# Neighbourhood attention: how q, k and v are laid out in scratch memory and loaded

## The chip, the cores and the metric

The kernel runs on one core of one Trainium2 chip. The metric is the device time of one execution in microseconds. The kernel before was run three times: 3532.39, 3535.32 and 3536.39 us, median 3535.32 us.

## What is computed

An encoder layer over two sequences, one of 512 tokens (prompt, s = 0) and one of 2048 (sample, s = 1), width 1024, all in float32. After a layer norm the input is projected by w_in into the operands of four mixers of width 256; their outputs are joined, projected by w_out, and followed by a layer norm, a feed-forward block with a convolution of width 3, and a last layer norm. The change touches the first mixer, neighbourhood attention: tokens stand on a grid with rows of 64, and each query attends to a window of 8 rows by 16 columns, with a bias by relative place.

```python
def _mixer(h, ...):
    z = h @ w_in
    ...
    o_a = _natten(qa.reshape(hs), ka.reshape(hs), va.reshape(hs), na_rpb)
    o_b = _fourier_mix(fb)
    o_c = _mla(cq, ckv, kr, mla_q_g, w_uq, mla_kv_g, w_ukv, cos, sin)
    o_d = _spatial_gating(sg, sgu_ln_g, sgu_ln_b, sgu_w, sgu_b)
    mix = jnp.concatenate([o_a, o_b, o_c, o_d], axis=-1)
    return mix @ w_out
```

## The kernel before, in words

The program runs in stages, and intermediate results pass between them through scratch tensors in HBM. To keep float32 precision, an operand x is split into a high part (rounded to fp32r) and a low part, x minus the high part; a product is then the sum of three matmuls, or of two in which both parts stand on 128 partitions, 64 for each. hi() at L126 and L130 and split() at L136 make the parts: L126 is ScalarE (ACT), L130 GpSimd (POOL), L136 VectorE (DVE) or POOL.

**First phase (phase1, 0 to about 500 us).** Five blocks of 512 tokens. feat() (L386) computes 128 features for a block: f 0 and 1 are q (two pairs of heads j), 2 and 3 are k, 6 and 7 feed the Fourier mixer. It empties PSUM into two tiles of the tag zs (four buffers), hi and lo, and stores them: q goes to zq[s][j] as three planes, hi, lo, hi; k to zk[s][j] as two planes. keyed() (L417) computes the values, tokens on the partitions, 128 tokens at a time, and stores one tile zs of 128 rows by 2 KB (both pairs, both heads, hi and lo) to zv[s].

**Attention stage.** From about 680 us natten() (L655) and mla() (L844, the third mixer) run woven together: the loop in build() takes three steps of natten for every four of mla. natten works in bands of eight grid rows of queries, two for the prompt and eight for the sample (s, j, i), and each band in eight units: four ranges of columns c (starting at CW = 0, 8, 24, 32, each 32 wide) by two heads hh. For a unit, scores() multiplies q by k (L708), adds the bias table and takes the maximum on DVE (L711), does the exponential on ACT and scales on POOL (L717); flip() transposes on TensorE (L726); values() multiplies by the values (L738, L739). The loads:

- band(): for each head hh, q is a tile of 128 partitions: partitions 0 to 63 hold one part, 64 to 127 the other. Two loads fill it (x = 0 straight, x = 1 with the parts exchanged, by taking planes x and x + 1 of the three); one load fills k (kt in the code, a tile of the arena, so a<-zk in the trace). The source pattern of each is 2 planes by 64 rows by columns. It is called six units ahead.
- window(): the values of one range of columns, in loads of 128 rows by 1 KB; the source pattern is 4 grid rows by 32 columns by 256 values. It is called two units ahead.
- table(): the bias table of a unit (L692 on), a load of 8 by 16 by n values from the scratch tensor R into one of six tiles tbl, then an addition of the mask on POOL at L697. It is called three units ahead; the ranges c = 1 and 2 share a table. The mask has one buffer and is loaded once a band.

In mla(), softmax() scales a row block of scores on POOL at L924, and turn() transposes it on TensorE at L936 afterwards. Its own loads go into a ring of three tiles raw.

**What sets the order.** Each engine works through its own instructions in order, in the order in which the program emits them and a scheduler places them. All loads and stores are issued by the SyncE queue (SP), through load() at L118 and store() at L121, so one that waits for a buffer, or whose issue takes long, holds all behind it.

Of the kernel before, what the change touches and what calls it, by code (L numbers as in the profile page):

```python
# [9 lines left out]
F32 = mybir.dt.float32  # L10
# [5 lines left out]
P = 128  # L16
D = 1024
KD = D // P
SEQS = ((0, 512), (1, 2048))
# [3 lines left out]
GRID_W = 64  # L23
# [8 lines left out]
CW = (0, 8, 24, 32)  # L32
# [74 lines left out]
class Builder:  # L107
# [65 lines left out]
    def build(self):  # L173
        tc, nc, I = self.tc, self.nc, self.I
        with tc.tile_pool(name="cst", bufs=1, reuse_waits="tile") as cst, tc.tile_pool(name="scr", bufs=1, space=bass.MemoryType.DRAM) as scr:
# [20 lines left out]

            d = lambda shape, tag: self.t(scr, shape, tag)
            self.y1 = [d([T, D], f"y1_{s}") for s, T in SEQS]
            self.zq = [[d([3, P, T], f"zq{s}_{j}") for j in range(2)] for s, T in SEQS]
            self.zk = [[d([2, P, T], f"zk{s}_{j}") for j in range(2)] for s, T in SEQS]  # L200
            self.zv = [d([T, 2, 2, 2, 64], f"zv{s}") for s, T in SEQS]
            self.zf = [[d([2, P, T], f"zf{s}_{j}") for j in range(2)] for s, T in SEQS]
            self.c = [d([3, P, T], f"c{s}") for s, T in SEQS]
            self.kr = [d([T, 32], f"kr_{s}") for s, T in SEQS]
# [64 lines left out]
    def phase1(self):  # L269
        tc, nc, I = self.tc, self.nc, self.I  # L270
        w_in = I["w_in"][0].rearrange("(k p) n -> p k n", p=P)
        with tc.tile_pool(name="p1w", bufs=1, reuse_waits="tile") as wp, tc.tile_pool(name="p1x", bufs=1, reuse_waits="tile") as xp, \
# [113 lines left out]
            def feat(b, f, uT):  # L386
                s, t0 = blocks[b]
                xh, xl = xT[b]
                ps = self.t(pp, [P, 512], "mm", bufs=4)
                for k in range(KD):  # L390
                    self.mm3(ps, wh[f][:, k], wl[f][:, k], xh[k], xl[k], k == 0, k == KD - 1)
                if f < 8:
                    hi = self.t(sp, [P, 512], "zs", F32R, bufs=ZS)
                    lo = self.t(sp, [P, 512], "zs", F32R, bufs=ZS)
                    j = f % 2
                    if f < 2:
                        src = ps.rearrange("p (r c q) -> p c r q", r=8, c=4, q=16)
                        dh, dl = [a.rearrange("p (c r q) -> p c r q", c=4, q=16)[:, :, ::-1, ::-1] for a in (hi, lo)]
                        self.split(src, dh, dl, "act", "dve")
                        dst = self.zq[s][j]  # L400
                    elif f < 4:
                        nc.scalar.activation(hi, ps, AF.Copy, scale=-0.125)
                        nc.vector.scalar_tensor_tensor(lo, ps, -0.125, hi.bitcast(F32), op0=ALU.mult, op1=ALU.subtract)
                        dst = self.zk[s][j]
                    else:
                        self.evac(ps, hi, lo)
                        dst = self.zf[s][j]
                    for i, a in enumerate((hi, lo, hi) if f < 2 else (hi, lo)):
                        self.store(dst[i, :, t0:t0 + 512], a.bitcast(F32))
                elif f < 11:  # L410
                    zs = self.t(sp, [P, 512], "zs", bufs=ZS)
                    nc.scalar.copy(zs, ps)
                    self.store(self.c[s][f - 8][:, t0:t0 + 512], zs)
                else:
                    nc.scalar.activation(uT[:, f - 11], ps, AF.Gelu_apprx_tanh)

            def keyed(b):  # L417
                s, t0 = blocks[b]
                xh, xl = xT[b]
                for t2 in range(2):  # L420
                    ps = self.t(pp, [P, 2, 2 * P], "mm", bufs=4)
                    for t in range(2):
                        tl = slice((2 * t2 + t) * P, (2 * t2 + t + 1) * P)
                        for k in range(KD):
                            self.mm3(ps[:, t], xh[k][:, tl], xl[k][:, tl], vh[:, k], vl[:, k], k == 0, k == KD - 1)
                    for t in range(2):
                        z = self.t(sp, [P, 2, 2, 2, 64], "zs", F32R, bufs=ZS)
                        src = ps[:, t].rearrange("p (j h d) -> p j h d", j=2, h=2)
                        self.split(src, z[:, :, :, 0], z[:, :, :, 1], "act", "dve")
                        r0 = t0 + (2 * t2 + t) * P  # L430
                        self.store(self.zv[s][r0:r0 + P].rearrange("p j h a d -> p (j h a d)"),
                                   z.bitcast(F32).rearrange("p j h a d -> p (j h a d)"))

            def keep_wout(k):
                wo = I["w_out"][0].rearrange("(k p) (a n) -> p k a n", p=P, a=2)
# [7 lines left out]
            def token(b):  # L443
                s, t0 = blocks[b]
                xh, xl = xT[b]
                v = self.t(xp, [P, 4, 4, 64], "uv", bufs=2)
                krs = self.t(sp, [P, 4, 32], "krs", bufs=1)
                vps = [self.t(pp, [P, 288], "mm", bufs=4) for _ in range(4)]
                for k in range(KD):
                    wk, wlk = wh[13][:, k], wl[13][:, k]  # L450
                    for t in range(4):
                        tl = slice(t * P, (t + 1) * P)
                        nc.tensor.matmul(vps[t], xh[k][:, tl], wk, start=k == 0, stop=False)
                        nc.tensor.matmul(vps[t], xh[k][:, tl], wlk, start=False, stop=False)
                        nc.tensor.matmul(vps[t], xl[k][:, tl], wk, start=False, stop=k == KD - 1)
                for t in range(4):
                    nc.scalar.activation(v[:, t].rearrange("p h d -> p (h d)"), vps[t][:, :256], AF.Gelu_apprx_tanh)
                    nc.scalar.copy(krs[:, t], vps[t][:, 256:288])
                self.store(self.kr[s][t0:t0 + 512].rearrange("(t p) e -> p t e", p=P), krs)
                return v  # L460
# [37 lines left out]
            for b in range(nb):  # L498
                uv = lambda: self.t(xp, [P, 2, 512], "uv", bufs=2)
                if b < nb - 1:  # L500
                    for f in range(3):
                        feat(b, f, None)
                    norm(b + 1)
                    feat(b, 3, None)
                    keyed(b)
                    for f in range(6, 11):
                        feat(b, f, None)
                        if b and wo:
                            keep_wout(wo.pop(0))
                    uT = uv()  # L510
                    for f in range(11, 13):
                        feat(b, f, uT)
                    v = token(b)
                    turn(b + 1)
                    gating(b, v, uT)
                else:
                    v = token(b)
                    uT = uv()
                    for f in range(11, 13):
                        feat(b, f, uT)  # L520
                    for f in range(2):
                        feat(b, f, None)
                    gating(b, v, uT)
                    for f in (2, 3):
                        feat(b, f, None)
                    keyed(b)
                    for f in range(6, 11):
                        feat(b, f, None)
# [126 lines left out]
    def natten(self, wp):  # L655
# [6 lines left out]
        half = (slice(0, 64), slice(64, P))  # L662

        def band(s, j, i):
            _, r0, nr = BANDS[s][i]
            n = nr * GRID_W
            kt = self.a((10, 12)[jobs.index((s, j, i)) % 2], [P, 2, 1024], F32R)
            for hh in range(2):
                q = self.t(wp, [P, 2, 4, P], "q", F32R, bufs=4)
                for x in range(2):  # L670
                    self.load(q[:, x].bitcast(F32).rearrange("p c q -> p (c q)"),
                              self.zq[s][j][x:x + 2, half[hh], i * 512:(i + 1) * 512])
                self.load(kt[:, hh, :n].bitcast(F32), self.zk[s][j][:, half[hh], r0 * GRID_W:r0 * GRID_W + n])
                qk[s, j, i, hh] = q, kt[:, hh]

        def window(s, j, i, c):
            _, r0, nr = BANDS[s][i]
            v = self.t(wp, [P, 4, 2, P], "vt", F32R, bufs=3)
            z = self.zv[s]
            for k in range(nr // 4):  # L680
                self.load(v[:, k].bitcast(F32).rearrange("p h d -> p (h d)"),
                          bass.AP(z.tensor, z.offset + ((r0 + 4 * k) * GRID_W + CW[c]) * 512 + j * 256,
                                  [[GRID_W * 512, 4], [512, 32], [1, 256]]))
            V[s, j, i, c] = v

        def table(s, j, i, c, hh):
# [65 lines left out]
        N, LAG = len(units), 2  # L752
        at = lambda f, x: f(units[x]) if 0 <= x < N else None
        band(*jobs[0])
        window(*units[0][:4])
        for x in range(3):
            table(*units[x])
# [833 lines left out]
```

## Time and profile before

| | |
|---|---|
| median of three runs | 3535.32 us |
| profiled execution, its own time | 3535.3 us |
| its span | 3533.5 us |
| busy: PE, DVE, ACT, POOL | 3141.0, 2119.8, 1375.6, 1620.1 us |
| mean granted clock of TensorE | 0.94 |
| moved by DMA | 653.42 MB, mean 185 GB/s |

The span is the time between the first and the last instruction recorded; the profiled execution's own time is 1.8 us longer. PE is TensorE's matmul, PEld its weight load. SPq is the SyncE queue: the time of one of its rows is that of issuing a DMA, not of moving the data. A matmul's recorded duration overlaps its neighbours' (they are pipelined), so counts of matmuls in a stretch say more of the pace than their durations. The granted clock is 1.00 at full speed (2.4 GHz) and 0.50 at the lower level (1.2 GHz); a value between is a mean over the stretch. The DMA share is the mean over the core's 16 DMA engines.

### The profile page before, as it was taken

To read this page: it belongs to the slowest core of one execution; us is meant where nothing else is said; L and a number is where in the kernel's file an instruction comes from. 1 tells how busy PE (TensorE), PEld (TensorE's weight loads), DVE (VectorE), ACT (ScalarE), POOL (GpSimd) and SP (SyncE) were. 2 spreads that over 40 slices of the span, in tenths; PEclk is the share of its full clock that TensorE was granted. 3 is DMA by queue.
4 is the path that set the end of the run, shared out by engine and by line. 5 is a ranking of instruction groups with operands and counts; after the bars stand their busy time and mean duration, and the time that the engine had idled before them with its cause. 6 is when DMAs were issued, how large, how long until landed. Compare 5 with 4: busy or idle time off the path is not lost. (4 is left out here: it accounts for less than half of the span.)

```text
span 3533.5 us, 46949 instructions
## 1 busy us (share of the span) xinstructions
PE 3141.0 (89%) x16375; PEld 2752.1 (78%) x16375; DVE 2119.8 (60%) x3802; ACT 1375.6 (39%) x2497; POOL 1620.1 (46%) x1360
## 2 busy tenths in 40 slices
PE   7999999555567666999999999999989999999997
PEld 6788888445566556888878998898979997787785
DVE  6333235444455455765478787666556556769678
ACT  3222234433344444652244444443344332225324
POOL 6322114423444333643378875655244213456546
PEclk9999999677788788999999999999999999999999
DMA  7354263222222222245466666999769867667653
GB/s 240 139 184 162 65 216 123 83 77 72 96 90 81 87 84 88 68 139 170 150 221 238 241 238 235 325 330 327 250 220 355 270 232 263 226 214 269 216 189 125
DMA packets 410432, 653.42 MB, mean 185 GB/s; under 512 B 50512, under 2 KB 266928, under 8 KB 409428
## 3 DMA queue, kind: packets, MB, share of 16 engines
q1 hardware_dynamic: 410196, 650.43, 53.5%
q8 instruction: 130, 2.13, 0.2%
q14 instruction: 106, 0.87, 0.1%
HBM read 437.31 MB, written 213.00 MB: 184 GB/s over the span
## 5 line engine op out<-in xcount | busy, mean ns | idle before, releaser
L136 POOL TENSOR_TENSOR w<-wraw,w 128x512 fp32r<-128x512 f32 x150 | 225.6, 1507 | 325.1 <-ACT w L126 281.1
L936 PE MATMUL t<-ident,a 128*128 128x128 f32 x1088 | 174.6, 292 | 138.1 <-POOL a L924 135.2
L908 DVE TENSOR_SCALAR_CACHE_REDUCE a<-s,low 128x512 f32<-128x512 f32 x272 | 195.3, 744 | 155.8 <-PE s L145 148.9
L1247 PE MATMUL s<-B,w 128*128 128x450 f32 (+1 forms) x792 | 284.7, 362 | 2.9 <-DVE h L1117 2.1
L1248 PE MATMUL s<-B,w 128*128 128x450 f32 (+1 forms) x792 | 286.1, 361 | 0.5 <-DVE B L136 0.5
L1248 PE MATMUL t<-T,w 128*128 128x450 f32 (+1 forms) x792 | 285.2, 360 | 0.0
L1247 PE MATMUL t<-T,w 128*128 128x450 f32 (+1 forms) x792 | 281.0, 360 | 3.9 <-DVE u L1117 3.5
L1249 PE MATMUL s<-B,w 128*128 128x450 f32 (+1 forms) x792 | 284.5, 359 | 0.0
L1249 PE MATMUL t<-T,w 128*128 128x450 f32 (+1 forms) x792 | 283.3, 358 | 0.0
L936 PEld LDWEIGHTS t<-ident,a 128*128 128x128 f32 x1088 | 138.9, 151 | 161.6 <-POOL a L924 138.8
L697 POOL TENSOR_TENSOR tbl<-tbl,mask 128x384 f32<-128x384 f32 (+2 forms) x60 | 63.2, 1056 | 393.9 <-DMA tbl<-R 355.8
L136 DVE TENSOR_TENSOR a<-t,a 128x512 fp32r<-128x512 f32 x240 | 160.1, 684 | 120.0 <-ACT a L126 118.4
L126 ACT CAST a<-t 128x512 fp32r<-128x512 f32 x240 | 136.1, 587 | 228.9 <-PE t L936 224.9
L1255 DVE SCALAR_TENSOR_TENSOR h<-h,convc,h 128x896 f32<-128x896 f32 (+1 forms) x132 | 221.5, 1708 | 0.0
L952 PE MATMUL o<-a,a 128*128 128x256 f32 x544 | 149.9, 301 | 56.7 <-ACT a L126 52.2
L1254 DVE SCALAR_TENSOR_TENSOR h<-h,convc,h 128x896 f32<-128x896 f32 (+1 forms) x132 | 166.5, 1292 | 54.0 <-ACT h L1253 54.0
L1453 PE MATMUL t<-w,go 128*128 128x512 f32 x696 | 194.8, 399 | 4.2 <-ACT go L126 1.8
L1253 ACT ACTIVATE h<-h,convc 128x896 f32<-128x896 f32 (+1 forms) x132 | 138.3, 1095 | 129.7 <-DVE h L1117 128.7
L144 PE MATMUL mm<-xTl,a 128*128 128x512 f32 x440 | 174.6, 397 | 1.5 <-DVE xTl L136 1.5
L953 PE MATMUL o<-a,a 128*128 128x256 f32 x544 | 155.2, 315 | 20.9 <-POOL a L136 20.5
L126 ACT CAST w<-wraw 128x512 fp32r<-128x512 f32 x154 | 94.9, 618 | 198.3 <-PE t L1249 135.7
L145 PE MATMUL mm<-xTh,a 128*128 128x512 f32 x440 | 171.2, 393 | 0.0
(366 smaller groups left out, 9363.4 us busy)
## 6 DMA issues: line engine op xcount, KB each, us to landing
w<-wuops SPq DMA_DIRECT2D x220, 512.0 KB
wuops<-w SPq DMA_DIRECT2D x110, 512.0 KB
w<-wdops SPq DMA_DIRECT2D x104, 512.0 KB
wraw<-in_w_up_dram SPq DMA_DIRECT2D x88, 512.0 KB
wdops<-xs SPq DMA_DIRECT2D x74, 512.0 KB
graw<-g SPq DMA_DIRECT2D x100, 256.0 KB
wd<-wdops SPq DMA_DIRECT2D x48, 512.0 KB
g<-h SPq DMA_DIRECT2D x44, 448.0 KB
```

Source lines behind the costliest of these rows:

```text
L126: nc.scalar.copy(out, src)
L136: e.tensor_tensor(lo, src, hi.bitcast(F32), op=ALU.subtract)
L144: mm(ps, wh, xl, start=False, stop=False)
L145: mm(ps, wl, xh, start=False, stop=last)
L908: nc.vector.tensor_scalar(e[:, c * 512:c * 512 + 512], ps, 1.0, self.low, op0=ALU.mult, op1=ALU.max, accum_out=m4[:, c:c + 1])
L936: nc.tensor.transpose(pt[:, k], e[:, kk * P:(kk + 1) * P], self.ident)
L1247: mm(ps[:, :hw], a, xh, start=first and k == 0, stop=False, skip_group_check=True)
L1248: mm(ps[:, :hw], a, xl, start=False, stop=False, skip_group_check=True)
L1249: mm(ps[:, :hw], b, xh, start=False, stop=last and k == KH - 1, skip_group_check=True)
L1254: nc.vector.scalar_tensor_tensor(c[:, :n], hb[:, 1:n + 1], cw[:, 1, ft:ft + 1], c[:, :n], op0=ALU.mult, op1=ALU.add)
L1255: nc.vector.scalar_tensor_tensor(c[:, :n], hb[:, 2:n + 2], cw[:, 2, ft:ft + 1], c[:, :n], op0=ALU.mult, op1=ALU.add)
L1453: mm = lambda a, b, st, sp_: nc.tensor.matmul(ps, a, b, start=st, stop=sp_, skip_group_check=True)
```

## The change

zq keeps two planes (hi, lo) in place of three. band() loads each half of 64 partitions by itself: four loads for a head's q, two for its k. zv is replaced by one scratch tensor for each range of columns c, whose rows stand in the order in which window() reads them: two grid rows (128 tokens) give 64 rows. keyed() stores each tile of values in eight pieces of 32 rows, one for each range and grid row; the ranges overlap. window() then loads 128 rows that lie one after the other.

```diff
--- before.py
+++ after.py
@@ -196,9 +196,9 @@
 
             d = lambda shape, tag: self.t(scr, shape, tag)
             self.y1 = [d([T, D], f"y1_{s}") for s, T in SEQS]
-            self.zq = [[d([3, P, T], f"zq{s}_{j}") for j in range(2)] for s, T in SEQS]
+            self.zq = [[d([2, P, T], f"zq{s}_{j}") for j in range(2)] for s, T in SEQS]
             self.zk = [[d([2, P, T], f"zk{s}_{j}") for j in range(2)] for s, T in SEQS]
-            self.zv = [d([T, 2, 2, 2, 64], f"zv{s}") for s, T in SEQS]
+            self.zv = [[d([T // 2, 2, 2, 2, 64], f"zv{s}_{c}") for c in range(4)] for s, T in SEQS]
             self.zf = [[d([2, P, T], f"zf{s}_{j}") for j in range(2)] for s, T in SEQS]
             self.c = [d([3, P, T], f"c{s}") for s, T in SEQS]
             self.kr = [d([T, 32], f"kr_{s}") for s, T in SEQS]
@@ -405,7 +405,7 @@
                     else:
                         self.evac(ps, hi, lo)
                         dst = self.zf[s][j]
-                    for i, a in enumerate((hi, lo, hi) if f < 2 else (hi, lo)):
+                    for i, a in enumerate((hi, lo)):
                         self.store(dst[i, :, t0:t0 + 512], a.bitcast(F32))
                 elif f < 11:
                     zs = self.t(sp, [P, 512], "zs", bufs=ZS)
@@ -427,9 +427,12 @@
                         z = self.t(sp, [P, 2, 2, 2, 64], "zs", F32R, bufs=ZS)
                         src = ps[:, t].rearrange("p (j h d) -> p j h d", j=2, h=2)
                         self.split(src, z[:, :, :, 0], z[:, :, :, 1], "act", "dve")
-                        r0 = t0 + (2 * t2 + t) * P
-                        self.store(self.zv[s][r0:r0 + P].rearrange("p j h a d -> p (j h a d)"),
-                                   z.bitcast(F32).rearrange("p j h a d -> p (j h a d)"))
+                        r0 = (t0 + (2 * t2 + t) * P) // 2
+                        zz = z.bitcast(F32).rearrange("p j h a d -> p (j h a d)")
+                        for c in range(4):
+                            for r in range(2):
+                                self.store(self.zv[s][c][r0 + 32 * r:r0 + 32 * r + 32].rearrange("p j h a d -> p (j h a d)"),
+                                           zz[64 * r + CW[c]:64 * r + CW[c] + 32])
 
             def keep_wout(k):
                 wo = I["w_out"][0].rearrange("(k p) (a n) -> p k a n", p=P, a=2)
@@ -667,20 +670,18 @@
             kt = self.a((10, 12)[jobs.index((s, j, i)) % 2], [P, 2, 1024], F32R)
             for hh in range(2):
                 q = self.t(wp, [P, 2, 4, P], "q", F32R, bufs=4)
-                for x in range(2):
-                    self.load(q[:, x].bitcast(F32).rearrange("p c q -> p (c q)"),
-                              self.zq[s][j][x:x + 2, half[hh], i * 512:(i + 1) * 512])
-                self.load(kt[:, hh, :n].bitcast(F32), self.zk[s][j][:, half[hh], r0 * GRID_W:r0 * GRID_W + n])
+                for a in range(2):
+                    for x in range(2):
+                        self.load(q[half[a], x].bitcast(F32).rearrange("p c q -> p (c q)"),
+                                  self.zq[s][j][a ^ x, half[hh], i * 512:(i + 1) * 512])
+                    self.load(kt[half[a], hh, :n].bitcast(F32), self.zk[s][j][a, half[hh], r0 * GRID_W:r0 * GRID_W + n])
                 qk[s, j, i, hh] = q, kt[:, hh]
 
         def window(s, j, i, c):
             _, r0, nr = BANDS[s][i]
             v = self.t(wp, [P, 4, 2, P], "vt", F32R, bufs=3)
-            z = self.zv[s]
             for k in range(nr // 4):
-                self.load(v[:, k].bitcast(F32).rearrange("p h d -> p (h d)"),
-                          bass.AP(z.tensor, z.offset + ((r0 + 4 * k) * GRID_W + CW[c]) * 512 + j * 256,
-                                  [[GRID_W * 512, 4], [512, 32], [1, 256]]))
+                self.load(v[:, k].bitcast(F32).rearrange("p h (a d) -> p h a d", a=2), self.zv[s][c][(r0 + 4 * k) * 32:(r0 + 4 * k + 4) * 32, j])
             V[s, j, i, c] = v
 
         def table(s, j, i, c, hh):
```

## Rows read from the trace of the kernel before

**Rows 1.** The page, the span in 40 slices of 88 us: busy tenths, granted clock.

```profile
PE   7999999555567666999999999999989999999997
...
PEclk9999999677788788999999999999999999999999
DMA  7354263222222222245466666999769867667653
```

**Rows 2.** Waits, 690 to 1470 us: who waited for whom; total us, times, longest.

```profile
POOL tbl L697 <- DMA tbl<-R: 355.8, 32, 37.6
...
PE t L936 <- POOL a L924: 135.2, 10, 31.2
```

**Rows 3.** Timeline of POOL: start, duration, instruction; in brackets idle time before, releaser.

```profile
710.47 2.90 POOL L697 TENSOR_TENSOR tbl<-tbl,mask 128x256 f32<-128x256 f32 x4 [25.85 <-DMA tbl<-R]
...
882.55 0.99 POOL L697 TENSOR_TENSOR tbl<-tbl,mask 128x384 f32<-128x384 f32 x1 [32.03 <-DMA tbl<-R]
...
1016.85 1.27 POOL L697 TENSOR_TENSOR tbl<-tbl,mask 128x512 f32<-128x512 f32 x1 [10.67 <-DMA tbl<-R]
...
1348.73 1.26 POOL L697 TENSOR_TENSOR tbl<-tbl,mask 128x512 f32<-128x512 f32 x1 [7.90 <-DMA tbl<-R]
...
1381.85 1.26 POOL L697 TENSOR_TENSOR tbl<-tbl,mask 128x512 f32<-128x512 f32 x1 [28.07 <-DMA tbl<-R]
```

**Rows 4.** Timeline of the SyncE queue, 840 to 866 us.

```profile
842.76 1.82 SPq L118 DMA_DIRECT2D a<-zk  x1
844.62 12.30 SPq L118 DMA_DIRECT2D q<-zq  x2
856.97 5.32 SPq L118 DMA_DIRECT2D a<-zk  x1
862.39 3.56 SPq L118 DMA_DIRECT2D tbl<-R  x1
```

**Rows 5.** Short windows: length, busy us and count by engine, granted clock, DMA share, GB/s.

```profile
850.00:856.00 6.00, 6.00 (x35) 5.42 (x34) 3.10 (x10) 1.82 (x6) 0.52 (x2) 0.72 0.13 52
...
868.00:874.00 6.00, 0.00 (x0) 0.00 (x0) 0.00 (x0) 0.00 (x0) 0.00 (x0) 0.50 0.26 90
...
1505.00:1520.00 15.00, 14.80 (x106) 13.40 (x105) 12.48 (x37) 10.37 (x15) 6.95 (x6) 1.00 1.00 385
```

**Rows 6.** Eight windows without band loads in the way: two of them, and the sum.

```profile
980.00:1020.00 40.00, 38.78 (x264) 34.97 (x263) 33.12 (x94) 27.53 (x52) 18.11 (x20) 0.96 0.27 90
1060.00:1082.00 22.00, 21.79 (x154) 19.57 (x153) 17.97 (x50) 16.60 (x30) 12.86 (x13) 1.00 0.29 84
...
sum 175.00, PE 171.54 PEld 154.22 DVE 147.26 ACT 127.43 POOL 91.41; mean PE 21.44 PEld 19.28 DVE 18.41 ACT 15.93 POOL 11.43
```

**Rows 7.** Timeline of PE near 1350 us.

```profile
1351.99 1.11 PE L936 MATMUL t<-ident,a 128*128 128x128 f32 x4 [7.58 <-POOL a L924]
```

**Rows 8.** Windows of the stage: its start, the whole of it, its tail.

```profile
690.00:745.00 55.00, 21.16 (x78) 15.32 (x78) 12.56 (x43) 10.04 (x20) 8.70 (x12) 0.59 0.27 84
690.00:1423.00 733.00, 461.56 (x2839) 404.98 (x2839) 361.15 (x1059) 312.47 (x602) 278.60 (x286) 0.79 0.26 85
...
1423.00:1500.00 77.00, 72.85 (x474) 64.91 (x472) 57.21 (x167) 51.69 (x98) 44.17 (x44) 0.93 0.20 59
```

**Rows 9.** By tile, issues on SP: ns min/median/max, first and last start.

```profile
L118 SPq DMA_DIRECT2D q<-zq x40: 500/2643/11733, 681.1 to 1351.7; - x40
...
L118 SPq DMA_DIRECT2D a<-zk x20: 495/1724/9567, 602.4 to 1358.2; - x20
...
L118 SPq DMA_DIRECT2D vt<-zv x128: 514/544/5074, 691.5 to 1464.4; - x128
...
L118 SPq DMA_DIRECT2D raw<-K x20: 445/492/4609, 620.7 to 1427.4; - x20
...
L121 SPq DMA_DIRECT2D zv<-zs x20: 319/352/3500, 58.9 to 469.1; - x20
```

**Rows 10.** Four windows of the first phase, 130 to 500 us: their sum.

```profile
sum 370.00, PE 365.70 PEld 318.61 DVE 125.39 ACT 84.99 POOL 88.59; mean PE 91.42 PEld 79.65 DVE 31.35 ACT 21.25 POOL 22.15
```

**Rows 11.** Timeline near 162 us, in keyed.

```profile
162.33 0.42 DVE L136 TENSOR_TENSOR zs<-mm,zs 128x256 fp32r<-128x256 f32 x1 [3.82 <-DMA zv<-zs]
```

## The prediction, written before the change was run

> **What bounds the kernel now.** I read four views in order: the slices of the page, the waits of one stretch, the timeline of the SyncE queue (SP) there, and the busy times in short windows. The slices show TensorE (PE) at nine tenths or so almost everywhere, except in slices 8 to 16, where its share falls to five to seven tenths and its granted clock to 0.6 to 0.8 [rows 1]. That is the stretch from 690 to 1423 us, in which natten runs woven into mla. PE does 2839 matmuls there in 733 us, busy for 461.56 us, at a mean clock of 0.79 [rows 8]. No other engine is full either: DVE 361 us, ACT 312, POOL 279. So the stage waits for something that is not an engine.
>
> The waits name it: POOL stood 355.8 us, in 32 waits of up to 37.6 us, in front of the addition at L697, for a bias table to land (tbl<-R) [rows 2]. POOL is in order, so the softmax scaling of mla at L924 stands behind that addition, and PE's transposes at L936 wait for L924 (135.2 us in ten waits [rows 2]). Nine of the POOL waits are over 20 us, about one per band of natten; [rows 3] has the first, a middle one and the last.
>
> Why a 192 to 256 KB table is late is seen on SP. Before the table of 862.39 us stand the loads of the next band: a<-zk, two q<-zq, a<-zk, which hold SP from 842.76 to 862.29 us [rows 4]. Meanwhile the 16 DMA engines are busy to a share of 0.13, at 52 GB/s; a little later to 0.26, at 90 GB/s; the same engines stand at 1.00 and 385 GB/s at 1505 us, when the weights of the next stage are loaded [rows 5]. 0.13 of 16 is two engines, 0.26 is four. The code fits: the source of q and of kt is a pattern whose outermost size is 2 (the halves), that of vt has outermost 4 (the grid rows), and the tables have 8. So I read the stretch as transfers that use as many DMA engines as their outermost size, with the table queued behind them on those engines.
>
> **The change, part by part.**
>
> *Loads of q and kt.* 40 loads of q become 80 and 20 of kt become 40, each of 64 rows with the rows outermost. The nearest row is raw<-K, which is 64 rows of 2 KB: it takes SP a median of 0.492 us to issue, against 2.643 us for q<-zq and 1.724 us for a<-zk [rows 9]. A band now has 12 such loads: 12 x 0.492 = 5.9 us of SP in place of the 19.5 us above, and the tables and mla's raw loads behind them on SP go out that much earlier. The band's 2 MB or so, at 385 GB/s, takes about 5.5 us; at the 52 GB/s of today it takes about 40.
>
> *Loads of vt.* The same 128 loads of 128 rows of 1 KB, now with the 128 rows outermost. SP's part was 0.544 us by the median [rows 9] and stays; the 0.26 share that they caused goes.
>
> *What the stage then costs.* I take the pace from the stretches of this very stage in which no band load was in the way. Eight such windows of 15 to 40 us, 175 us in all, hold 1206 matmuls by the sum of their counts (264 and 154 in the two shown): 6.89 per us, with PE busy for 171.54 of 175 us, DVE for 147 [rows 6]. The matmuls of the stage are unchanged, so 2839 / 6.89 = 412 us. Two things are added. The start: today 690 to 745 us holds only 78 matmuls [rows 8], worth 11 us at that pace. After the change the first twelve loads, two vt, the mask and the first tables must still come before the first scores; I take 15 us lost, between 5 and the 44 of today. Remaining stalls: after the last table, at 1423 to 1500 us, natten and mla run with no tables and no band loads at 474 matmuls in 77 us, 6.16 per us [rows 8]; at that pace the stage takes 461 us, 49 more. The truth lies between the best windows and this tail; I take the middle, 25 us. Stage: 412 + 15 + 25 = 452 us for 733, a gain of 281.
>
> *What is late next.* In the good windows PE is at 98% and DVE at 84%, so PE is the bound, with the granted clock at 1.00 once the gaps are gone. Short table waits on POOL stay: 10.67 us before 1016.85 cost PE next to nothing, as that window has PE at 38.78 of 40 us [rows 3, 6]; but the 7.90 us before 1348.73, close upon another, came out as a PE wait of 7.58 us before 1351.99 [rows 3, 7]. That is what the 25 us are for.
>
> *Stores of the first phase.* keyed stored 20 tiles of values once each (zv<-zs, median 0.352 us of SP [rows 9]); it now stores each in eight pieces of 32 rows, 160 in all, twice the bytes because the column ranges overlap. Ten stores of zq go. Net 130 more issues; at 0.352 us that is 46 us of SP over five blocks. Per block, 32 pieces take 11.3 us. Behind them on SP stand the y1 stores and the stores of zf, and behind those the four zs buffers, whose release lets ACT and DVE empty the next PSUM tile. What hides it is that PE sets this phase (365.70 of 370 us busy [rows 10]), with four PSUM banks of slack: even the 3.82 us that DVE waited for a zv store to give back its buffer [rows 11] left PE full. If that cover goes, the price is up to 46 us; below nothing only if the ten dropped zq stores free buffers sooner. I take 3 us, nearest to the row that cost nothing.
>
> **The sum.** The profiled execution took 3535.3 us, on the median of the runs (3535.32). 3535.3 - 733 + 452 + 3 = 3257 us. Best ends: no stall, 5 us of start, no cost in the first phase: 3535.3 - 733 + 417 = 3219, and 8 us less if the tail after 1423 us also takes the good pace (474 / 6.89 = 69 us for 77): 3211.
>
> **A rule that speaks against it.** The rows: one load over both halves keeps only two of sixteen engines busy [rows 5]. The Trainium skill, DMA: Bandwidth & Descriptors, section "Rules for kernel authors", says not to bother with two transfers to disjoint partition halves, since both halves use all 16 engines anyway, and to use one transfer of 128 partitions; by that rule the time would be that of rival B. The same page, in the section on why a DMA increments its semaphore by 16, lets the slowest dimension of both patterns set the number of engines, so that the whole load here would use 2 and the half 16; by that the sum stands. The 0.13 agrees with the second and contradicts the reason given in the first.
>
> **Rivals.**
>
> A. *The tables stay late, though less.* Twelve loads of 2 MB now fill all engines, and the table behind them still waits for them, some 10 us longer at each of the nine places, too long for POOL's slack. For it: the 7.90 us that cost 7.58 [rows 3, 7]. Against: 10.67 us that cost nothing. Price 9 x 10 = 90 us on the forecast: 3347 us.
>
> B. *Halves gain nothing.* Only vt gets faster. Of a stall of about 28 us, the 18 us in which q and kt hold SP at a share of 0.13 [rows 4, 5] stay, some 10 us go: 9 x 10 = 90 us, 3445 us. Against it stands raw<-K, a half that SP issues in 0.492 us among the same traffic.
>
> C. *SP becomes the bound of the first phase.* If a piece of 32 rows took as long to issue as q<-zq now (2.643 us), the 130 net issues would be 344 us of SP in a phase where PE has next to no idle time: 3257 + 344 = 3601 us, slower than before. It outweighs the gain of 278 us from 2.1 us an issue. For it: one zv store took 3.5 us; against: the median of 0.352 [rows 9].
>
> D. *The loads still run on few engines*, because something other than the outermost size decides. Then only the 3 us of stores remain: 3538 us, no change. Against: 0.13 and 0.26 fit sizes 2 and 4 too well for chance.
>
> **How the numbers follow.** Forecast 0.75, A 0.17, B 0.04, C 0.02, D 0.02. A difference of 0.2%, 7 us, is about what a measurement of this kernel can tell from no change; forecast, A and B are faster, D the same, C slower: 0.96, 0.02, 0.02. The range goes from the best ends, 3211, to rival A, 3347.
>
> **What would show it.** Right: POOL's waits for tbl<-R falling from 355.8 us to under 100; q<-zq and a<-zk issued in about half a microsecond each; no stretch of 10 us in natten with PE idle and the DMA share near 0.13; the last L697 near 1140 us in place of 1423; the first phase within 3 us of its length. Wrong: waits over 20 us at L697 that stay (B, D; under D the share of 0.13 stays with them), waits near 10 us that come out on PE (A), or ACT and DVE waiting for zv stores with gaps on PE before 500 us (C). A stage at 6.2 matmuls per us without table waits would mean that the pace of the good windows was too kind.

## The result, and the profile after

The changed kernel takes 3233.19 us (median of three runs, 3224.74 to 3241.02) for 3535.32 before: a ratio of 0.9146, 95% interval 0.9108 to 0.9184. Run again five times beside later experiments it took 3229.19 us, ratio 0.9134 (0.9122 to 0.9146). The forecast was 3257 us, in a range of 3211 to 3347. The profiled execution shown below is the slowest of the three, 3241.02 us with a span of 3239.2.

The page of the kernel after, the same lines as in [rows 1]; a slice is now 81 us:

```profile
PE   7999999889999999999999999999899999999997
...
PEclk9999999889999999999999999999899999999999
DMA  6454345354545433446666679987698776647652
```

The valley of slices 8 to 16 has gone; what is left is a notch in slices 8 and 9, where the prompt's mla and the start of natten stand. The granted clock has come up with PE: nothing was done to it.

Windows of the kernel after: a short one among a band's loads, the whole stage (from 8.9 us after the first load of q, as in [rows 8], to the last table addition), the 55 us that held 78 matmuls before, and the tail.

```profile
683.50:1127.30 443.80, 424.78 (x2830) 374.19 (x2830) 356.14 (x1055) 311.96 (x602) 279.58 (x287) 0.97 0.50 140
690.00:745.00 55.00, 49.88 (x315) 42.09 (x313) 41.71 (x136) 37.11 (x76) 33.86 (x41) 0.96 0.51 136
...
1127.30:1204.00 76.70, 73.61 (x487) 65.22 (x486) 59.49 (x170) 52.19 (x100) 45.35 (x46) 0.96 0.20 59
...
868.00:874.00 6.00, 6.00 (x46) 5.54 (x45) 5.35 (x18) 4.11 (x9) 2.83 (x3) 1.00 0.99 222
```

733 us have become 443.8 for the same matmuls (2839 and 2830 recorded): 6.38 per us. The last of the four lines answers to [rows 5]: among a band's loads the DMA share was 0.13 to 0.26 with PE at rest at the worst; now it is 0.99 for some microseconds, with PE full.

Waits of the kernel after, 670 to 1240 us, and its longest wait for a table on POOL's timeline (the lines of the file have moved by one: L698 is L697 of before):

```profile
POOL tbl L698 <- DMA tbl<-R: 74.2, 27, 8.1
```

```profile
963.01 1.02 POOL L698 TENSOR_TENSOR tbl<-tbl,mask 128x384 f32<-128x384 f32 x1 [8.03 <-DMA tbl<-R]
```

355.8 us have become 74.2, and the longest wait 8.1 us in place of 37.6 [rows 2, 3]. PE's waits for the transposes behind L924 are no longer among the longest of the stage. On SP the loads of a band are issued without a hold; its timeline at the loads of one band, answering to [rows 4]:

```profile
862.18 3.38 SPq L118 DMA_DIRECT2D q<-zq  x4
865.67 0.53 SPq L118 DMA_DIRECT2D raw<-Q  x1
866.30 0.62 SPq L118 DMA_DIRECT2D tbl<-R  x1
866.97 0.44 SPq L118 DMA_DIRECT2D raw<-Q  x1
867.46 1.10 SPq L118 DMA_DIRECT2D a<-zk  x2
868.66 1.95 SPq L118 DMA_DIRECT2D vt<-zv  x4
871.05 1.09 SPq L118 DMA_DIRECT2D q<-zq  x2
872.18 0.59 SPq L118 DMA_DIRECT2D a<-zk  x1
873.11 1.08 SPq L118 DMA_DIRECT2D q<-zq  x2
874.24 0.59 SPq L118 DMA_DIRECT2D a<-zk  x1
874.93 1.43 SPq L118 DMA_DIRECT2D tbl<-R  x2
```

By tile, the issues on SP after (ns min/median/max), which answer to [rows 9]:

```profile
L118 SPq DMA_DIRECT2D q<-zq x80: 444/594/1612, 674.6 to 1075.7; - x80
...
L118 SPq DMA_DIRECT2D a<-zk x40: 444/594/1063, 604.4 to 1076.4; - x40
...
L118 SPq DMA_DIRECT2D vt<-zv x128: 315/428/681, 680.4 to 1165.4; - x128
...
L121 SPq DMA_DIRECT2D zv<-zs x160: 303/427/1831, 62.5 to 478.0; - x160
```

The table additions of the kernel after, from the first to the last:

```profile
L698 POOL TENSOR_TENSOR tbl<-tbl,mask x60: 718/1017/1312, 686.7 to 1127.3; 128x384 f32<-128x384 f32 x24, 128x512 f32<-128x512 f32 x24, 128x256 f32<-128x256 f32 x12
```

Where the gain lies in the profiled execution (294.3 us of span): natten's first load comes 6.5 us earlier (674.6 for 681.1); from there to the last table addition (1127.3 for 1423.2) 452.7 us for 742.1, which is 289.4; from that to natten's last score 2.8; the rest of the kernel is 4.4 us longer, in an execution 8 us above the median.

### The profile page after: what moved, and what is told of

The parts are those of the page before. It is cut to its first block, busy times and chain, and to the rows that moved or that the text cites. A ratio compares the mean times of both kernels' runs of the same rounds, so it can differ in the third digit from the quotient of the medians.

```text
span 3239.2 us, 47194 instructions
## 1 busy us (share of the span) xinstructions
PE 3109.1 (96%) x16375; PEld 2727.4 (84%) x16375; DVE 2118.9 (65%) x3802; ACT 1376.2 (42%) x2497; POOL 1621.2 (50%) x1360
## 4 chain that ended last, share of the span: by engine, by line
PE 43%; DVE 4%; DMA 2%; issue 1%; POOL 1%; ACT 1%; SPq 0%; DVEq 0%; POOLq 0%; ACTq 0%
PE s L1248 6%; PE s L1249 6%; PE s L1250 6%; PE t L1454 5%; PE t L1248 4%; PE t L1249 4%; PE t L1250 4%; PE s L1454 4%; PE o L1454 3%; DMA graw<-g 1%; DVE go L136 1%; DVE x L1321 1%; POOL w L136 1%; DMA wraw<-x 1%; DMA w<-wdops 0%
## 5 line engine op out<-in xcount | busy, mean ns | idle before, releaser
L143 PE MATMUL mm<-xTh,a 128*128 128x512 f32 x440 | 168.9, 397 | 6.2 <-DVE ln0mv L159 5.0
L145 PE MATMUL mm<-xTh,a 128*128 128x512 f32 x440 | 171.9, 394 | 0.0
L937 PE MATMUL t<-ident,a 128*128 128x128 f32 x1088 | 162.7, 278 | 3.3 <-DVE a L136 1.6
L1454 PEld LDWEIGHTS t<-w,go 128*128 128x128 f32 x696 | 131.1, 189 | 38.8 <-DVE x L1321 4.2
L1248 PEld LDWEIGHTS t<-T,w 128*128 128x128 f32 x792 | 150.0, 189 | 16.3 <-DVE u L1118 4.2
L126 ACT CAST go<-gs 128x256 fp32r<-128x256 f32 x200 | 78.1, 405 | 195.9 <-PE t L1454 69.6
```

Source lines behind the costliest of these rows:

```text
L126: nc.scalar.copy(out, src)
L143: mm(ps, wh, xh, start=first, stop=False)
L145: mm(ps, wl, xh, start=False, stop=last)
L1248: mm(ps[:, :hw], a, xh, start=first and k == 0, stop=False, skip_group_check=True)
L1454: mm = lambda a, b, st, sp_: nc.tensor.matmul(ps, a, b, start=st, stop=sp_, skip_group_check=True)
```

## The experiments

**One part of the change at a time.** The first two kernels are the kernel before with one half of the diff each; the first has the new band() and two planes of zq, the second the new keyed(), zv and window().

> Kernel before with the q and k part alone (two planes of zq, each half loaded by itself); values stored and loaded as before. Theory (a load uses as many DMA engines as its outermost size, and the tables queue behind on them): the q and k loads, on two engines, were the long blockade; vt on four engines leaves some 5 us before a table, mostly hidden. Time 3240 to 3300 us, POOL's wait for the tables 80 to 160 us, no wait over 15 us. Rival B (halves gain nothing, only the values part does): 3520 to 3540 us, waits of 20 to 37 us stay.

> Kernel before with the values part alone (stored per range of columns, loaded with 128 rows outermost); q and k as before. Theory: q and k keep two engines busy for some 18 us and more per band, so the long waits stay, shorter by the share of vt: 3400 to 3480 us. Rival B (the whole gain is the values'): 3230 to 3250 us.

Measured on the same chip, with 3537.01 us for the kernel before: 3278.23 us with the q and k part, within what was expected, and 3489.95 with the values part, 10 us above it. Each ran once, and so did the kernels of the next part; the kernel after itself lay between 3224.55 and 3241.02 us in eight runs, so that 10 us between two single runs say little. Their waits, 660 to 1480 us:

```profile
POOL tbl L698 <- DMA tbl<-R: 118.1, 30, 10.9
```

```profile
POOL tbl L697 <- DMA tbl<-R: 341.8, 37, 33.9
```

The first line is that of the q and k part: the long waits have gone with q and k alone. The second is that of the values part: 14 us less waiting than before. Rival B is out on both sides. The gains, 259 and 47 us, add up to 306; the whole change has 304. The values part gained less than expected (57 us at the least); why was not tried. It is worth about the same in either order: 47 us added to the kernel before, and 49 from the q and k part alone (3278.23) to the kernel after run again (3229.19).

**Only the outermost size.** Two kernels are the kernel after with the access pattern of one kind of load made coarse again, at the same number of transfers, bytes and row length.

```diff
-self.zq[s][j][a ^ x, half[hh], i * 512:(i + 1) * 512]
+self.zq[s][j][a ^ x, half[hh], i * 512:(i + 1) * 512].rearrange("(r g) t -> g r t", g=2)
-self.zk[s][j][a, half[hh], r0 * GRID_W:r0 * GRID_W + n]
+self.zk[s][j][a, half[hh], r0 * GRID_W:r0 * GRID_W + n].rearrange("(r g) t -> g r t", g=2)
```

Rows of q and k are permuted alike, so their products are the same. The other one pads zv and reads it in four groups:

```diff
-self.zv = [[d([T // 2, 2, 2, 2, 64], f"zv{s}_{c}") for c in range(4)] for s, T in SEQS]
+self.zv = [[d([T // 64, 40, 2, 2, 2, 64], f"zv{s}_{c}") for c in range(4)] for s, T in SEQS]
...
+bass.AP(z.tensor, z.offset + (r0 + 4 * k) * 40 * 512 + j * 256, [[40 * 512, 4], [512, 32], [1, 256]])
```

> Kernel after, with one thing changed: every half of q and k is read from memory as 2 groups of 32 rows (even rows, odd rows) in place of 64 rows, the same permutation for q and k. Same number of transfers, same bytes, same row length, same destination, halves still by themselves; only the outermost size is 2 and no longer 64. Theory: back to two engines for q and k, so like the values part alone, 3400 to 3480 us, with POOL waits of 20 us and more at each band and stretches with a DMA share near 0.13. Rival (it is the splitting into halves, or the shorter transfers, that helped): stays at 3225 to 3245 us.

> Kernel after, with one thing changed: the scratch tensors of the values have a gap of 8 rows after each 32, so that a load's source is again 4 groups of 32 rows; stores, number of loads and bytes are those of after. Theory: vt back on four engines, like the q and k part alone: within 15 us of that run, 3240 to 3300 us. Rival (the order of the values in memory helped, not the outermost size): stays at 3225 to 3245 us.

Measured: 3481.19 us with q and k at 2 (1 us above what was expected), 3279.55 with the values at 4. The second is 1.3 us from the q and k part alone: order in memory and eight stores show no worth of their own in these two runs, and the outermost size by itself brings back what the values part had gained. The first gives back 252 of the 304 us while the halves stay apart. Its waits, and a window among its band loads:

```profile
POOL tbl L698 <- DMA tbl<-R: 342.7, 34, 35.2
```

```profile
850.00:856.00 6.00, 0.00 (x0) 0.00 (x0) 0.00 (x0) 0.00 (x0) 0.00 (x0) 0.50 0.13 51
```

Again 0.13 of sixteen engines, 51 GB/s, and every engine at rest. The same edit with 4 and 8 groups, one run each, gives the dose:

> As the run in which each half of q and k was read as 2 groups of 32 rows (3481 us), with 4 groups of 16 rows. Theory (engines = outermost size): the blockade of a band is half as long, some 10 us; of the 250 us that 2 groups cost, 25 to 45% stay: 3290 to 3345 us. Rival (any grouping, not its number, makes the load slow): 3450 to 3490 us; rival (only 2 is special): 3225 to 3245 us.

> The same with 8 groups of 8 rows. Theory: the blockade is a quarter, some 5 us, within what POOL's slack hides: 3230 to 3270 us. Rival (any grouping makes it slow): 3450 to 3490 us.

| outermost size of each half of q and k | us | POOL's wait for tables, longest |
|---|---|---|
| 2 | 3481.19 | 342.7, 35.2 |
| 4 | 3315.63 | 182.0, 15.6 |
| 8 | 3239.80 | 124.7, 10.2 |
| 64 (kernel after, run again) | 3229.19 | 95.1, 8.1 |

Both fall into the theory's range. The number of engines can be read off directly. Windows among the q and k loads, of the run at 4 and of the run at 8:

```profile
848.00:852.00 4.00, 0.45 (x2) 0.29 (x2) 2.56 (x8) 0.01 (x1) 4.00 (x4) 1.00 0.26 98
```

```profile
882.00:885.00 3.00, 3.00 (x24) 2.73 (x23) 1.03 (x4) 2.98 (x5) 3.00 (x4) 1.00 0.54 189
```

With 0.13 and 51 GB/s at size 2, the share is about 2, 4 and 8 sixteenths, and the rate 24 to 26 GB/s for each engine so counted.

The excess over the kernel after is 252, 86 and 11 us; the last is not clear of the spread of the kernel after. It falls faster than the blockade halves, and no fixed slack that hides the first 10 us of each wait explains it: the run at 4 has eight waits over 10 us, which pass 10 us by 21 us in all, and it lost 86. How much of that is a lower clock after the gaps (a mean granted clock of 0.969 in that run, for 0.980) was not separated. The total of POOL's waits comes closer: 248, 87 and 30 us more than the 95.1 of the kernel after (74.2 in its other profiled execution). It is not the whole price either: the q and k part alone has 118.1 us of such waits, fewer than the run at 8, and took 38 us longer. What late values cost besides was not tried.

**Whole transfers, other layouts.** With the kernel after as their measure on the same chip:

> The kernel after, unchanged, on the same chip as the next three, as their measure: 3225 to 3245 us.

It took 3229.19 us. Next, q and k stored in the order of the loads, so that one load covers both halves:

```diff
+for h in range(2):
+    src = a[64 * h:64 * h + 64].bitcast(F32)
+    for x in range(2 if f < 2 else 1):
+        r = 64 * (i ^ x)
+        to = dst[h, x] if f < 2 else dst[h]
+        self.store(to[r:r + 64, t0:t0 + 512], src)
...
+self.load(q[:, x].bitcast(F32).rearrange("p c q -> p (c q)"), self.zq[s][j][hh, x, :, i * 512:(i + 1) * 512])
+self.load(kt[:, hh, :n].bitcast(F32), self.zk[s][j][hh, :, r0 * GRID_W:r0 * GRID_W + n])
```

> Kernel after, but q and k are stored in the order in which the loads want them (q twice, once per arrangement), so that a load is one transfer over both halves again, 128 rows with the rows outermost: 40 loads of q and 20 of k, as before the change, and 60 more stores in the first phase. Theory (outermost size decides, halves as such do not matter): within 15 us of the kernel after. Rival (short transfers of a half are what let the tables through): POOL waits over 20 us return, 3400 us or more.

3245.39 us (ratio 0.9183, 0.9167 to 0.9198): 16 us more than the kernel after, 1 us outside what was expected. But the stage itself is the same: from the first load of q to the last score 688.7 to 1182.6, 493.9 us, for 671.3 to 1165.1, 493.8 us, in the kernel after run again. So halves as such gain nothing and lose nothing. The 16 us were lost in the first phase, where 80 stores of 64 rows for q and 40 for k stand in place of 20 and 20 (80 more, not the 60 of the expectation). ACT and DVE waited 55 us there for such stores to give back a zs buffer, for 4 us in the kernel after run again. Its last store, in the kernel after run again, and in this one (timelines of SP):

```profile
492.10 0.33 SPq L121 DMA_DIRECT2D c<-zs  x1
```

```profile
508.56 0.33 SPq L121 DMA_DIRECT2D c<-zs  x1
```

The variant with both arrangements of q in one load (20 loads of q and 20 of k, for 120):

> The version with q and k stored in the order of the loads, and both arrangements of q in one load: 20 loads of q, 20 of k, 128 rows outermost, for 120 in the kernel after. Theory: SP has some 40 us less to issue in the stage, but SP is not what the stage waits for now; within 15 us of the kernel after, faster if the table waits (74.2 us) shrink. Rival (SP's issue time is the next bound): 20 to 40 us faster than the kernel after.

3243.94 us (0.9176, 0.9164 to 0.9189), with 490.9 us from first load to last score: 3 us better in the stage, 14 us worse in the first phase, in one execution each. So 80 loads fewer on SP bought next to nothing there. Then the values stored as before and loaded by grid rows:

```diff
+for g in range(4):
+    t0 = (r0 + 4 * k + g) * GRID_W + CW[c]
+    self.load(v[32 * g:32 * g + 32, k].bitcast(F32).rearrange("p h (a d) -> p h a d", a=2), self.zv[s][t0:t0 + 32, j])
```

> Kernel after, but the values are stored as before the change (20 stores, one tensor) and each load of 128 rows becomes four of 32 rows, one per grid row, with the rows outermost: 512 loads for 128. Theory (outermost size decides, order in memory does not): no wait over 15 us for a table; SP issues some 384 loads more, at 0.33 us some 127 us of the 450 us of the stage, which puts 16 issues in place of 4 ahead of a table (5 us for 1.7): 0 to 40 us more than the kernel after. Rival (the order in memory, whole runs of 128 rows, helped): as the q and k part alone, 3270 to 3290 us or worse, with the values' loads slow. A first phase shorter by up to 4 us would show the price of the eight stores.

3247.91 us (0.9189, 0.9176 to 0.9202), 19 us more than the kernel after and no wait for a table above 11.0 us. So the order of zv in memory is not what lets the tables through; what it saves is 384 loads. The stage took 516.0 us for 493.8, with 512 loads of a median of 419 ns in place of 128 of 424. That these issues are what cost the 22 us fits, but was not shown. No table wait explains them: those fell to 56.4 us. The first phase did not get shorter without the eight stores (its last store at 497.42 us for 492.10).

**Which queue.** In the kernel before, the tables alone were given to ScalarE's queue:

```diff
-self.load(t[:, :n], bass.AP(self.R.tensor, ...))
+nc.scalar.dma_start(t[:, :n], bass.AP(self.R.tensor, ...))
```

> Kernel before, with one thing changed: the 60 table loads are issued from ScalarE's queue in place of SP's; q, k and values are loaded as before, on few engines. If a table is late because SP issues it late and it then stands in the same queue on the two or four busy engines, a queue of its own gets it through in turn: waits at L697 mostly under 10 us, 3300 to 3450 us (mla's own loads stay behind q and k on SP). If it is late because those engines have no time left for it whatever the queue: waits of 20 us and more stay, 3500 to 3560 us.

3537.51 us in one run, beside 3537.82 for the kernel before: by the time, the second case; by the waits for tables, the first. Its waits, 660 to 1480 us:

```profile
POOL tbl L697 <- DMA mask<-in_na_mask_dram: 152.1, 7, 30.0
POOL tbl L697 <- DMA tbl<-R: 125.4, 30, 12.8
PE o L952 <- ACT a L126: 117.5, 9, 29.8
...
POOL Q L130 <- DMA raw<-Q: 96.7, 10, 33.7
```

POOL waited less for tables (125.4 us for 355.8, 12.8 at the longest), while q, k and values still went over few engines. Once issued from ACT's queue, a table got through: where POOL waited for one (30 of 60), its addition began at most 8.3 us after the start of its issue, for up to 21.1 us in the kernel before. The longest of these waits, on the timelines of SP's queue, ACT's queue and POOL:

```profile
1350.85 12.41 SPq L118 DMA_DIRECT2D q<-zq  x2
```

```profile
1352.32 0.58 ACTq L696 DMA_DIRECT2D tbl<-R  x1
```

```profile
1360.51 1.28 POOL L697 TENSOR_TENSOR tbl<-tbl,mask 128x512 f32<-128x512 f32 x1 [12.78 <-DMA tbl<-R]
```

Two things took the tables' place. What else stood late in SP's queue was next: the mask, which stands in front of the same addition, and mla's queries. And ACT, whose queue the tables now used, stood still in front of its own table issues: 145 us in 16 gaps of over 1 us, here 18.8 us before the issue at 1059.50:

```profile
1040.45 0.26 ACT L745 COPY hb<-o 64x128 f32<-64x128 f32 x1
1059.50 0.58 ACTq L696 DMA_DIRECT2D tbl<-R  x1
```

PE's waits for ACT at L952 rose to 117.5 us from 52.2. What held those issues was not tried. So the tables were late because of the queue in which they stood, behind transfers that only few engines worked on. Moving this one victim, at the price of ACT's time, was worth 0 us where the cause removed was worth 304; what the late tables alone cost, this run does not tell.

**The waits that are left.** The tables of the kernel after, fetched two units earlier:

```diff
-if x + 3 < N:
-    table(*units[x + 3])
+if x + 5 < N:
+    table(*units[x + 5])
```

> Kernel after, with tables fetched five units ahead in place of three (six buffers as before). If the POOL waits that are left (74 to 95 us in all, 8 us at most) still cost something, 5 to 20 us less than the kernel after (3229 us, ratio 0.913 to before); if POOL's slack hides them, as the forecast has it for most, no difference beyond 5 us. The addition moves ahead with the load, so POOL can meet the load just as early as now: then the waits stay too.

3233.27 us (0.9140, 0.9126 to 0.9154) for 3229.19 (0.9134): no difference that the runs can tell, with 87.8 us of waits for 95.1. As the addition moves with its load, the waits did not fall, so this does not say what their removal would be worth. No version tried beats the kernel after.

## Why the prediction was right

**The bound.** The chain from few engines by way of late tables and an in-order POOL to an idle PE was read from the waits and two DMA shares. The runs at 2, 4, 8 and 64 show its two ends: the outermost size sets the share, and the time follows. That it runs by way of the tables is shown less well: the waits of POOL fall with the time in these runs, and the run with the tables on another queue shows why they were late; but that run gained nothing, as others then stood late and ACT was held, so the price of the tables' lateness by itself stays open. The Trainium skill, DMA: Bandwidth & Descriptors, section on why a DMA increments its semaphore by 16, says that the slowest dimension of both patterns sets the number of engines; the trace agrees, with shares of 0.13, 0.26 and 0.54 at sizes 2, 4 and 8, and 0.99 when rows are outermost.

**The rule against it.** The Trainium skill, DMA: Bandwidth & Descriptors, section "Rules for kernel authors", advises against two transfers to the two halves of the partitions. Here that holds in one sense: whole transfers with the rows outermost took 493.9 us for the stage, halves 493.8. It does not hold for the load of before, whose two halves were its outermost dimension: splitting that one was worth 259 us.

**The terms.** The stage was forecast at 452 us and took 443.8. From where the start ends, at 745 us:

```profile
745.00:1127.30 382.30, 370.11 (x2509) 329.28 (x2507) 311.93 (x914) 274.25 (x524) 243.58 (x244) 0.98 0.49 139
```

Here it ran at 2509 / 382.3 = 6.56 matmuls per us, between the good pace of 6.89, which it did not hold, and the 6.16 of the tail; the tail itself now has 487 in 76.7 us, 6.35. The stalls that stay are 382.3 - 2509 / 6.89 = 18 us, for 25. The start, 61.5 us with the other 321 matmuls, lost 61.5 - 321 / 6.89 = 15 us, for 15. The pace came from rows; the 15 and the 25 were choices inside wide bounds (5 to 44, 0 to 49), so that the sum came out within 8 us is partly luck. The price of a single wait was not settled: the 10.67 us that cost PE nothing do not stand for every wait of that length, as the run at 4 shows.

**The first phase** was put at 3 us and had 0.9 (its last store at 494.89 us for 493.98, in one execution each). That DMA waits for zs buffers would be hidden was right, though they grew: 36.6 us on DVE and 23.7 on ACT for zv stores, where 3.8 us stood before. That the price is 0 was a matter of number, not of kind: 80 more stores of q and k cost 16 us.

```profile
DVE zs L136 <- DMA zv<-zs: 36.6, 8, 9.3
...
ACT zs L126 <- DMA zv<-zs: 23.7, 5, 8.0
```

These are waits of the kernel after, 40 to 510 us.

**Issue times.** I took 0.492 us for a half, from raw<-K, and it is 0.594; for vt I left 0.544 and it is 0.428; for a piece of 32 rows 0.352 and it is 0.427. None of it decides: 80 loads fewer on SP took 3 us off the stage.

**What was off.** The time is 24 to 28 us better than the forecast (3233 and 3229 for 3257). In the profiled execution, 3241 us, the 16 us are 8 in the stage, 2 in the first phase, 7 between the last store of that phase and natten's first load (179.7 us for 187.1), and 3 from the last table to the last score, less 4 in the rest. The 7 us lie in a stretch that the prediction left out, and they have the same cause: k of the next band is loaded there too. Before, two such loads are issued at 645.39 us, and PE then stands; after, it does not:

```profile
654.00:660.00 6.00, 0.00 (x0) 0.00 (x0) 0.00 (x0) 0.65 (x2) 0.22 (x1) 0.64 0.15 53
```

```profile
654.00:660.00 6.00, 5.50 (x39) 4.92 (x38) 5.81 (x20) 5.53 (x13) 3.77 (x6) 1.00 0.43 111
```

The stretch takes 186 to 188 us in the four kernels that load q and k at an outermost size of 2 (before, values alone, size 2, tables on ACT's queue), and 176 to 181 in the nine other profiled executions.

**The rivals.** A stood on waits of 10 us longer per band coming out on PE; the longest wait is 8.1 us. B fell with the first two runs, C with a median of 0.427 us per issue, D with the shares.

## What to carry to other kernels

When a stage stands still while DMA shows a small, flat share, read that share as a number of engines (0.13 of 16 is two) and look for a load whose outermost dimension has that size; rows outermost, at the same bytes and even the same number of transfers, was worth 252 us here. The load that is late need not be the slow one: the tables were behind it in the queue, and moving them alone, to ACT's queue, bought nothing. Price a removed stall by the pace of the same stage's undisturbed windows, found before the change, and allow for a mean somewhat below it: 6.56 matmuls per us here for 6.89.

## What was not expected

Halving the number of engines did not double the price: 2 engines for q and k cost 252 us, 4 cost 86, and 8 cost 11, which a single run cannot tell from nothing. A free 10 us in each wait does not explain it; the total of POOL's waits follows it more closely. And a load issued from another queue got through to busy engines: with SP's loads on few engines, tables from ScalarE's queue were there within 8.3 us of their issue, where in SP's queue it took up to 21.1. The time stayed all the same: the mask stood late in their place, and ACT was held in front of its own issues.
